# A gated-delta scan whose TensorE order is written out in the program, one product of the output projection between two blocks

## The chip, the core and the metric

The kernel runs on one core of a Trainium2 chip. The metric is device microseconds of one execution, median of several runs. TensorE multiplies (its 128x128 stationary operand is loaded by a LDWEIGHTS that the profile lists as PEld), VectorE (DVE) and ScalarE (ACT) read the results out of PSUM, GpSimd (POOL) works on SBUF alone, and SyncE (SP) issues the DMAs. Each engine works through its own instructions in the order in which they stand in the program and stops at the first that has to wait for a semaphore.

## The reference, cut to what matters

Two layers: banded attention, then gated DeltaNet, each followed by a gated output projection. The change touches only the chunked recurrence of the second layer and the projection that follows it, for 16 value heads of width 128, 64 tokens in a chunk, 33 chunks (16 tokens in the first):

```python
v_new = u - jnp.einsum('bhcd,bhdv->bhcv', w, S)
o = (jnp.einsum('bhcd,bhdv->bhcv', qc * jnp.exp(gcum)[..., None], S)
     + jnp.einsum('bhcs,bhsv->bhcv', attn, v_new))
S = S * jnp.exp(g_last)[..., None, None] + jnp.einsum('bhcd,bhcv->bhdv', k_state, v_new)
...
o = rms_norm(o, o_norm_w) * jax.nn.silu(z.reshape(B, L, DN_V_HEADS, DN_HEAD_DIM_V))
return o.reshape(B, L, DN_VALUE_WIDTH) @ w_out
```

## The kernel before

The program has four stages: projections of the attention layer, attention, projections of the DeltaNet layer, and `dn_scan`, which the change edits. The keys, values and small triangular matrices of every chunk have been written to DRAM by then.

`dn_scan` walks over 33 chunks `ng` and, within a chunk, over 4 pairs `gp` of key-head groups: 132 items, `seq`. An item passes through three stages. `stage0` multiplies the state S with keys and queries of the pair (tile `r`, two matmuls, one for each group j); POOL then scales S, DVE makes `xp` out of the key half of `r` and ACT makes `qs` out of its query half, each in four pieces (j, h). `stage1` multiplies `xp` with the inverted triangle `tp` (tile `vn`, two matmuls; the first needs the first two pieces of `xp`, the second the last two), and ACT copies it to `vs`. `stage2` makes the update of the state out of `vs` (tile `ds`, added to S by DVE) and the output (tile `o`, added to `qs` by DVE into `osb`, squared by ACT into `ssq`). After the fourth pair of a chunk `post` takes the reciprocal root on DVE (`m_o`, then ten operations on 128x8: `f_o`, `rsq_t`), scales `osb` on POOL, transposes it (tile `tp_o`, twice four) and lets DVE multiply it with z into `ot`. After two chunks (128 tokens) `ot` is complete, and a job of `out_proj` is queued: ACT and DVE split `ot` into a high and a low half (`oh`, `ol`, four parts each), 48 matmuls of 512 columns run into the tile `ps_o` (16 heads by three products, `mm3`, lines 61 to 63), and DVE adds the residual `h_t`. This is the projection's first half of columns; the second half runs after the scan from the stored `ot`. Below, a product of the projection is one of these 48 matmuls.

A step t of the loop runs `stage0` of item t, `stage1` of item t-1 and `stage2` of item t-2, and `project()` twice, each of which moves the job by one head (three products). So the code has r of item t+1 ahead of vn of item t. The tiles `vn`, `ds`, `o`, `ps_o` have one PSUM buffer, `r` has two.

The order in which instructions stand on the engines is not the order of the code: the program is built with `schedule_with_timeline_sim=True`, and the scheduler moves an instruction ahead or back on its engine wherever the data allow it.

Of the kernel before, what the change touches and what calls it, by code (L numbers as in the profile page):

```python
# [1041 lines left out]
def dn_scan(tc, a, out, sc, ident, pers):  # L1042
    nc = tc.nc
    v = nc.vector
    w_out = a["dn_w_out"][0]
    with (
        tc.tile_pool(name="pBw", reuse_waits="tile", bufs=1) as wp,
        tc.tile_pool(name="pBc", reuse_waits="tile", bufs=1) as cp,
# [20 lines left out]
        def out_proj(i, c, w, ot, tag="po"):  # L1069

            parts = []
            for q in range(4):
                oh = lp.tile([P, 4, P], F32R, tag="oh", bufs=4, name="oh2")
                ol = lp.tile([P, 4, P], F32R, tag="ol", bufs=4, name="ol2")
                split(nc, oh, ol, ot[:, q * 4:q * 4 + 4, :])
                parts.append((oh, ol))
            ht = lp.tile([P, 512], F32, tag="ht", name="h_t2")
            nc.sync.dma_start(ht, sc["h1"][NMETA + i * P:NMETA + (i + 1) * P, c * 512:c * 512 + 512])
            ps = (vpp if tag == "o" else pp).tile([P, 512], F32, tag=tag, bufs=1, name="ps_o2")
            for h in range(NV):  # L1080
                oh, ol = parts[h // 4]
# [5 lines left out]
            yield  # L1087

        S = cp.tile([P, GH, 2, P], F32, tag="S", name="S")
        nc.gpsimd.memset(S, 0.0)  # L1090
# [13 lines left out]
        def load(ng):  # L1104
# [38 lines left out]
        def stage0(ng, gp):  # L1143

            hf, n = where(ng)
            kq, bv, kt, ap, tp, osb, ssq = loaded[ng]
            gs = slice(gp * 2, gp * 2 + 2)
            if ng == 0:
                live[ng, gp] = [bv[:, gs, :], None]
                return  # L1150
            r = rpp.tile([P, 2, 2, P], F32, tag="r", bufs=2, name="r_ps")
            for j in range(2):
                nc.tensor.matmul(r[:, j], lhsT=kq[:, gp * 2 + j, :], rhs=S[:, gp * 2 + j], start=True, stop=True)  # L1153
            if ng < 32:
                for j in range(2):
                    g = gp * 2 + j
                    nc.gpsimd.tensor_tensor(S[:, g], S[:, g],  # L1157
                                            pers["eL"][hf][:, :, g, n].unsqueeze(2).to_broadcast([P, 2, P]), op=ALU.mult)
            xp = sp.tile([P, 2, P], F32, tag="xp", bufs=3, name="xp")
            qs = sp.tile([P, 2, P], F32, tag="qs", bufs=4, name="qs")  # L1160
            for j in range(2):
                g = gp * 2 + j
                for h in range(2):
                    v.scalar_tensor_tensor(xp[hb[h], j], in0=r[0:64, j, h, :], scalar=pers["c1"][hf][hb[h], g, n:n + 1],  # L1164
                                           in1=bv[hb[h], g, :], op0=ALU.mult, op1=ALU.add)
                    nc.scalar.activation(qs[hb[h], j], r[64:128, j, h, :], AF.Copy,  # L1166
                                         scale=pers["ea"][hf][hb[h], g, n:n + 1])
            live[ng, gp] = [xp, qs]

        def stage1(ng, gp):  # L1170
            tp = loaded[ng][4]
            xp = live[ng, gp][0]
            vn = vpp.tile([P, 2, P], F32, tag="vn", bufs=1, name="vn_ps")
            for j in range(2):
                nc.tensor.matmul(vn[:, j], lhsT=tp[:, gp * 2 + j, :], rhs=xp[:, j], start=True, stop=True)  # L1175
            vs = sp.tile([P, 2, P], F32, tag="vs", bufs=3, name="vs")
            nc.scalar.copy(vs, vn)
            live[ng, gp].append(vs)

        def stage2(ng, gp):  # L1180
# [3 lines left out]
            if ng < 32:  # L1184
                ds = dpp.tile([P, 2, 4, P], F32, tag="ds", bufs=1, name="ds_ps")
                for j in range(2):
                    for h in range(2):
                        nc.tensor.matmul(ds[:, h, j, :], lhsT=kt[hb[h], gp * 2 + j, :], rhs=vs[hb[h], j],  # L1188
                                         start=True, stop=True)
                v.tensor_tensor(S[:, gs], S[:, gs], ds[:, :, 0:2, :].rearrange("p h j d -> p j h d"), op=ALU.add)  # L1190
            if ng:
                ops = vpp.tile([P, 2, P], F32, tag="o", bufs=1, name="o_ps")
                for j in range(2):
                    nc.tensor.matmul(ops[:, j], lhsT=ap[:, gp * 2 + j, :], rhs=vs[:, j], start=True, stop=True)  # L1194
# [5 lines left out]
        def post(ng, gg):  # L1200
# [15 lines left out]
            for q in range(gs.start // 4, gs.stop // 4):  # L1216
                t = pp.tile([P, 8, 64], F32, tag="tp", bufs=1, name="tp_o")
                for j in range(4):
                    nc.tensor.transpose(t[:, 2 * j:2 * j + 2, :], osb[:, q * 4 + j, :], ident)
# [3 lines left out]
                yield  # L1223
            if second and gg != 0:
                nc.sync.dma_start(sc["ot"][i], ot)
                ready.append(out_proj(i, 0, w0, ot))

        ready = []
        posts = []
# [3 lines left out]
        load_wo(0, w0)  # L1233
        seq = [(ng, gp) for ng in range(33) for gp in range(GH // 2)]

        def project():
            if ready and next(ready[0], 1):
                ready.pop(0)

        LAG = 1  # L1240
        for t in range(len(seq) + 2 * LAG):
            if t < len(seq):
                ng, gp = seq[t]
                if gp == 2 and ng + 2 < 33:
                    load(ng + 2)
                stage0(ng, gp)
            project()
            if 0 <= t - LAG < len(seq):
                stage1(*seq[t - LAG])
            if 0 <= t - 2 * LAG < len(seq):  # L1250
                ng, gp = seq[t - 2 * LAG]
                stage2(ng, gp)
                if ng == 32 and gp % 2:
                    posts.append(post(ng, gp // 2))
                elif ng and gp == GH // 2 - 1:
                    posts.append(post(ng, None))
                else:
                    for _ in range(2):
                        if posts and next(posts[0], 1):
                            posts.pop(0)  # L1260
            project()
        for p in posts:
            for _ in p:
                pass
        for p in ready:
            for _ in p:
                pass

# [3 lines left out]
        w1 += [lp.tile([P, 2, 512], F32R, tag="osb", name="wo2")]  # L1272
        load_wo(1, w1)
        for i in range(NXT):
            pool, tag = ((cp, "S"), (lp, "z"), (lp, "ot"))[i % 3]
            ot = pool.tile([P, NV, P], F32, tag=tag, bufs=1, name="ot")
            nc.sync.dma_start(ot, sc["ot"][i])
            for _ in out_proj(i, 1, w1, ot, "o" if i % 2 else "po"):
                pass


# [77 lines left out]
```

## Time and profile before

| what | us |
|---|---|
| median of 3 runs (lowest, highest) | 3184.79 (3182.53, 3192.68) |
| the profiled execution | 3190.57 |
| its span | 3187.9 |
| first to last `r` (the scan's steps) | 2374.2 to 2975.2 |
| first product of the projection | 2443.1 |
| eight steps (one job of the projection) in the middle of the scan | 36.95 |

Times in the rows are microseconds from the span's start. In the view in order of time a row holds its start, its duration, the engine, the line, and written tile<-read tiles; neighbours of one kind are merged (x4 are four records), and what the engine waited for stands in brackets. A matmul of fp32 operands leaves two records, so r has four, each half of vn two, ds eight and o four. A matmul row's duration runs to the end of its result; the next matmul begins before that, and what TensorE spends on a block is the distance to the next block's start.

### The profile page before, as it was taken

How to read it: one execution, taken by the hardware profiler on the slowest of the kernel's cores; microseconds unless marked ns; L12 is line 12 of the kernel's file. 1: busy time of each engine (PE TensorE's matmuls, PEld its weight loads, DVE VectorE, ACT ScalarE, POOL GpSimd, SP SyncE). 2: the span in 40 equal slices, each digit the busy share in tenths (PEclk: the TensorE clock that was granted, in tenths of full speed). 3: DMA queues.
4: the chain of work that ended last, by engine and by line, in shares of the span. 5: the costliest groups of instructions: out<-in, count | busy, mean ns of one | idle time of the engine just before them, and what ended most of it. 6: DMA issues, size and time to landing. Idle time of an engine off the chain costs nothing.

```text
span 3187.9 us, 53874 instructions
## 1 busy us (share of the span) xinstructions
PE 2959.2 (93%) x18685; PEld 2652.4 (83%) x18685; DVE 2215.7 (70%) x5836; ACT 1453.3 (46%) x4115; POOL 966.7 (30%) x1111
## 2 busy tenths in 40 slices
PE   7999998888887999988999999999998999999899
PEld 6999996766666999988999999998986777777687
DVE  6786028889988676796654777987328888777632
ACT  5514147666665535334323535342225555555421
POOL 2001004544544323231111323222126544444200
PEclk9999999999999999999999999999998999999999
DMA  4323123222223254446542445367446676766442
GB/s 119 104 66 99 62 83 92 77 72 74 65 63 115 70 128 109 112 115 157 161 122 72 122 103 149 87 153 200 123 122 180 178 183 175 200 173 164 155 139 99
DMA packets 556696, 385.89 MB, mean 121 GB/s; under 512 B 248504, under 2 KB 508472, under 8 KB 549256
## 3 DMA queue, kind: packets, MB, share of 16 engines
q1 hardware_dynamic: 520472, 365.66, 41.2%
q10 hardware_dynamic: 35952, 16.80, 1.9%
q8 instruction: 148, 2.42, 0.3%
q14 instruction: 124, 1.02, 0.1%
HBM read 245.38 MB, written 136.97 MB: 120 GB/s over the span
## 4 chain that ended last, share of the span: by engine, by line
PE 41%; DVE 18%; DMA 4%; ACT 3%; issue 2%; SPq 1%; POOL 1%; ACTq 0%; DVEq 0%; POOLq 0%
PE ps_d L61 6%; PE ps_d L62 6%; PE ps_d L63 6%; PE ps_o L63 4%; PE ps_o L61 4%; PE ps_o L62 4%; DVE acc L769 3%; PE r_ps L1153 2%; DVE Xt L936 2%; PE ds_ps L1188 2%; DVE X L938 2%; PE o_ps L1194 1%; DVE xp L1164 1%; PE vn_ps L1175 1%; DVE wi_lo L57 1%
## 5 line engine op out<-in xcount | busy, mean ns | idle before, releaser
L61 PE MATMUL ps_d<-y_hi,wi_hi 128*128 128x384 f32 (+2 forms) x2304 | 754.9, 328 | 34.0 <-ACT u L761 29.5
L63 PE MATMUL ps_d<-y_hi,wi_lo 128*128 128x384 f32 (+2 forms) x2304 | 743.6, 323 | 0.0
L62 PE MATMUL ps_d<-y_lo,wi_hi 128*128 128x384 f32 (+2 forms) x2304 | 743.6, 323 | 0.0
L61 PEld LDWEIGHTS ps_d<-y_hi,wi_hi 128*128 128x128 f32 x2304 | 440.9, 191 | 49.0 <-ACT u L761 34.8
L63 PEld LDWEIGHTS ps_d<-y_hi,wi_lo 128*128 128x128 f32 x2304 | 440.6, 191 | 3.5 <-issue 3.3
L62 PEld LDWEIGHTS ps_d<-y_lo,wi_hi 128*128 128x128 f32 x2304 | 440.4, 191 | 3.1 <-issue 2.9
L640 POOL TENSOR_TENSOR wi_raw<-wi_raw,nw 128x1024 f32<-128x1024 f32 x96 | 207.3, 2160 | 682.3 <-DMA wi_raw<-in_dn_w_in 587.7
L769 DVE SCALAR_TENSOR_TENSOR acc<-u,cw,acc 128x1040 f32<-128x1040 f32 (+1 forms) x192 | 292.0, 1521 | 6.1
L57 DVE TENSOR_TENSOR wi_lo<-wi_raw,wi_hi 128x1024 fp32r<-128x1024 f32 x96 | 120.5, 1255 | 204.0 <-ACT wi_hi L56 195.7
L1166 ACT ACTIVATE qs<-r_ps,ea 64x128 f32<-64x128 f32 x512 | 179.5, 362 | 143.9 <-DVE xp L1164 138.3
L1164 DVE SCALAR_TENSOR_TENSOR xp<-r_ps,c,bv_t 64x128 f32<-64x128 f32 x512 | 171.9, 342 | 78.9 <-ACT qs L1166 45.8
L1157 POOL TENSOR_TENSOR S<-S,eL 128x256 f32<-128x256 f32 x248 | 162.0, 673 | 183.1 <-PE r_ps L1153 173.7
L61 PE MATMUL ps_o<-wo,oh 128*128 128x512 f32 x512 | 209.6, 409 | 3.7 <-ACT oh L56 2.9
L63 PE MATMUL ps_o<-wo,ol 128*128 128x512 f32 x512 | 205.5, 401 | 0.0
L62 PE MATMUL ps_o<-wo,oh 128*128 128x512 f32 x512 | 205.3, 401 | 0.0
L61 PE MATMUL ps_mm<-w_hi,y_hi 128*128 128x256 f32 (+1 forms) x680 | 194.1, 288 | 10.7 <-ACT y_hi L103 4.6
L63 PE MATMUL ps_mm<-w_hi,y_lo 128*128 128x256 f32 (+1 forms) x680 | 194.7, 288 | 2.0 <-DVE y_lo L104 2.0
L62 PE MATMUL ps_mm<-w_lo,y_hi 128*128 128x256 f32 (+1 forms) x680 | 193.4, 286 | 0.3 <-DVE w_lo L57 0.3
L761 ACT COPY u<-ps_d 128x384 f32<-128x384 f32 (+2 forms) x192 | 84.8, 442 | 235.9 <-PE ps_d L63 235.4
L405 ACT ACTIVATE p<-p,nb 128x272 f32<-128x272 f32 (+2 forms) x272 | 133.8, 494 | 55.5 <-DVE nb L400 55.1
L56 ACT CAST wi_hi<-wi_raw 128x1024 fp32r<-128x1024 f32 x96 | 100.6, 1048 | 118.0 <-PE ps_d L62 95.9
L57 DVE TENSOR_TENSOR ol<-ot,oh 128x512 fp32r<-128x512 f32 x128 | 89.2, 699 | 91.8 <-ACT oh L56 91.8
(306 smaller groups left out, 7110.6 us busy)
## 6 DMA issues: line engine op xcount, KB each, us to landing
wi_raw<-in_dn_w_in SPq DMA_DIRECT2D x96, 512.0 KB, 4.0
kq_t<-d_kq SPq DMA_DIRECT2D x33, 512.0 KB, 8.1
bv_t<-d_bv SPq DMA_DIRECT2D x33, 512.0 KB, 4.6
x_t<-in_x SPq DMA_DIRECT2D x32, 512.0 KB, 3.7
d_kq<-kq SPq DMA_DIRECT2D x16, 1024.0 KB, 5.3
d_bv<-bv SPq DMA_DIRECT2D x32, 512.0 KB, 4.9
kt_t<-d_ktok SPq DMA_DIRECT2D x64, 256.0 KB, 4.2
z_t<-d_z SPq DMA_DIRECT2D x16, 1024.0 KB, 6.6
```

The lines of the kernel that those rows point to most:

```text
L56: nc.scalar.copy(hi, src)
L57: nc.vector.tensor_tensor(lo, src, hi.bitcast(F32), op=ALU.subtract)
L61: nc.tensor.matmul(ps, lhsT=lh, rhs=rh, start=start, stop=False)
L62: nc.tensor.matmul(ps, lhsT=lh, rhs=rl, start=False, stop=False)
L63: nc.tensor.matmul(ps, lhsT=ll, rhs=rh, start=False, stop=stop)
L405: nc.scalar.activation(p4[:n, hh, k0:272], p4[:n, hh, k0:272], AF.Exp, bias=nb[:n, hh:hh + 1], scale=SLOPES[hg * 4 + hh], accum_out=z[:n, ...
L640: nc.gpsimd.tensor_tensor(raw, raw, nw.unsqueeze(2).to_broadcast([P, KT, P]), op=ALU.mult)
L761: nc.scalar.copy(u[:, 3 + t0:3 + t0 + n], ps[:, :n])
L769: v.scalar_tensor_tensor(acc[:, :ncol], in0=u[:, j:j + ncol], scalar=cw[:, ct, j:j + 1], in1=acc[:, :ncol], op0=ALU.mult, op1=ALU.add)
L1157: nc.gpsimd.tensor_tensor(S[:, g], S[:, g], pers["eL"][hf][:, :, g, n].unsqueeze(2).to_broadcast([P, 2, P]), op=ALU.mult)
L1164: v.scalar_tensor_tensor(xp[hb[h], j], in0=r[0:64, j, h, :], scalar=pers["c1"][hf][hb[h], g, n:n + 1], in1=bv[hb[h], g, :], op0=ALU.mult, ...
L1166: nc.scalar.activation(qs[hb[h], j], r[64:128, j, h, :], AF.Copy, scale=pers["ea"][hf][hb[h], g, n:n + 1])
```

## The change

A local `matmul` marks every matmul of the scan with `tc.keep_in_program_order` from the fifth step on: the scheduler then has to leave TensorE's order as the code has it. The code's order within a step is turned round: `stage2` of item t-2, `stage1` of t-1, `stage0` of t. `project(1)` now moves the job by one product, and stands between any two of the blocks ds, o, vn, r and the transposes; a seventh one is added while two jobs are queued. The splits are taken out of the job's start: `split_out` does a quarter of the next job whenever the current one has done another 12 products. z gets two buffers. `post` gives up its second `yield`, and its two pieces run in the first steps of the next chunk. Its first steps (t up to 3) and what follows the scan stay with the scheduler. `post`'s and `out_proj`'s arithmetic is the same, and so is the number of every instruction.

```diff
+    def matmul(out, lhsT, rhs, start=True, stop=True):
+        ins = nc.tensor.matmul(out, lhsT=lhsT, rhs=rhs, start=start, stop=stop)
+        if fixed[0]:
+            tc.keep_in_program_order(ins)
...
+            for _ in range(delay):
+                yield
...
-                mm3(nc, ps, oh[:, h % 4, :], ol[:, h % 4, :], w[h][:, 0, :], w[h][:, 1, :], h == 0, h == NV - 1)
-                if h < NV - 1:
-                    yield
+                for j, (o, hl) in enumerate([(oh, 0), (oh, 1), (ol, 0)]):
+                    matmul(ps, o[:, h % 4, :], w[h][:, hl, :], h + j == 0, h == NV - 1 and j == 2)
+                    job["done"] += 1
+                    if h < NV - 1 or j < 2:
+                        yield
...
-                zt = lp.tile([P, NV, P], F32, tag="z", bufs=1, name="z_t")
+                zt = lp.tile([P, NV, P], F32, tag="z", bufs=2, name="z_t")
...
                 v.tensor_tensor(S[:, gs], S[:, gs], ds[:, :, 0:2, :].rearrange("p h j d -> p j h d"), op=ALU.add)
+            project(1)
             if ng:
                 ops = vpp.tile([P, 2, P], F32, tag="o", bufs=1, name="o_ps")
...
+        def project(n):
+            for _ in range(n):
+                if ready and next(ready[0][1], 1):
+                    ready.pop(0)
+                if len(ready) > 1:
+                    for q in range(ready[0][0]["done"] // 12):
+                        split_out(ready[1][0], q)
+
+        for t in range(len(seq) + 2):
+            fixed[0] = t > 3
+            project(1)
+            if t >= 2:
+                stage2(*seq[t - 2])
+            project(1)
+            if 1 <= t <= len(seq):
+                stage1(*seq[t - 1])
+            project(1)
             if t < len(seq):
                 ng, gp = seq[t]
...
                 stage0(ng, gp)
-            project()
-            if 0 <= t - LAG < len(seq):
-                stage1(*seq[t - LAG])
-            if 0 <= t - 2 * LAG < len(seq):
...
+            project(1)
...
+            project(2 if len(ready) > 1 else 1)
```

On TensorE, in the middle of the scan, this stood before; the number after a name tells buffers apart, and xp_28383 is made from r_28378, which stands just ahead of these rows, xp_28444 from r_28439:

```order
L1153 MATMUL r_ps_28439<-S_26493,kq_t_27925 128x256 x2
L1194 MATMUL o_ps_28407<-vs_28338,apad_26495 128x128 x2
L1175 MATMUL vn_ps_28457<-xp_28383,tpad_26501 128x128
L1188 MATMUL ds_ps_28462<-vs_28399,kt_t_27929 128x128 x4
L1194 MATMUL o_ps_28468<-vs_28399,apad_26495 128x128 x2
L1175 MATMUL vn_ps_28457<-xp_28383,tpad_26501 128x128
L1153 MATMUL r_ps_28486<-S_26493,kq_t_28152 128x256 x2
L1175 MATMUL vn_ps_28506<-xp_28444,tpad_26501 128x128
```

The r of the next item stood ahead of both halves of an item's vn, the halves stood apart, and the projection ran in bursts elsewhere. Now the same place reads so, on TensorE (xp_28388 is made from r_28383):

```order
L1050 MATMUL r_ps_28383<-S_26493,kq_t_27928 128x256 x2
L1050 MATMUL ps_o2_28228<-wo6_26513,oh2_28118 128x512
L1050 MATMUL ps_o2_28228<-wo6_26513,ol2_28119 128x512
L1050 MATMUL ps_o2_28228<-wo7_26514,oh2_28118 128x512
L1050 MATMUL ds_ps_28416<-vs_28359,kt_t_27932 128x128 x4
L1050 MATMUL ps_o2_28228<-wo7_26514,oh2_28118 128x512
L1050 MATMUL o_ps_28423<-vs_28359,apad_26495 128x128 x2
L1050 MATMUL ps_o2_28228<-wo7_26514,ol2_28119 128x512
L1050 MATMUL vn_ps_28432<-xp_28388,tpad_26501 128x128 x2
L1050 MATMUL ps_o2_28228<-wo8_26515,oh2_28122 128x512
L1050 MATMUL r_ps_28438<-S_26493,kq_t_27928 128x256 x2
```

Between an item's r and its vn stand three products, ds, a product, o, a product, and no other r; the next r stands behind the vn. VectorE, whose order is still the scheduler's, had before, for two items (xp in pieces, S and osb of earlier items):

```order
L1164 SCALAR_TENSOR_TENSOR xp_30010<-r_ps_30005,c11_12658,bv_t_29655 64x128 x3
L1222 TENSOR_TENSOR ot_29239<-tp_o_29931,z_t_29237 128x8x64
L1164 SCALAR_TENSOR_TENSOR xp_30010<-r_ps_30005,c11_12658,bv_t_29655 64x128
L1190 TENSOR_TENSOR S_26493<-S_26493,ds_ps_30028 128x512
L1195 TENSOR_TENSOR osb_29445<-o_ps_30034,qs_29888 128x256
```

and has now, for the item of the rows above:

```order
L1186 SCALAR_TENSOR_TENSOR xp_28388<-r_ps_28383,c10_12657,bv_t_27930 64x128 x2
L1211 TENSOR_TENSOR S_26493<-S_26493,ds_ps_28416 128x512
L1186 SCALAR_TENSOR_TENSOR xp_28388<-r_ps_28383,c10_12657,bv_t_27930 64x128
L1217 TENSOR_TENSOR osb_27947<-o_ps_28423,qs_28322 128x256
L1186 SCALAR_TENSOR_TENSOR xp_28388<-r_ps_28383,c10_12657,bv_t_27930 64x128
```

S and osb moved in between the second and the fourth piece of xp. Behind the last small block of the scan stand 855 products of the projection, where 816 stood.

## Rows read from the trace of the kernel before

**Rows 1.** Tiles of the scan: records, shortest/median/longest ns, first and last start.

```profile
L1153 PE MATMUL r_ps<-S,kq_t x512: 377/379/767, 2374.2 to 2975.2; 128*128 128x256 f32 x171
...
L61 PE MATMUL ps_o<-wo,oh x512: 389/392/795, 2443.1 to 3183.2; 128*128 128x512 f32 x171
```

**Rows 2.** The chain that ended last, 2600 to 2900 us: start, us, what.

```profile
2622.16 1.10 PE r_ps L1153 x4
...
2659.11 1.10 PE r_ps L1153 x4
```

**Rows 3.** Stretches: length, busy us (PE, PEld, DVE, ACT, POOL), clock, DMA share, GB/s.

```profile
2622.16:2659.11 36.95, 35.14 (x224) 28.79 (x225) 29.50 (x81) 21.54 (x77) 18.38 (x21) 1.00 0.67 182
...
3000.00:3187.90 187.90, 181.78 (x800) 149.35 (x798) 56.42 (x84) 40.76 (x66) 0.00 (x0) 1.00 0.39 135
```

**Rows 4.** Order of time, two items of the scan, all engines.

```profile
2720.74 0.71 PE L1188 MATMUL ds_ps<-vs,kt_t 64*128 64x128 f32 x8
...
2721.38 0.71 PE L1194 MATMUL o_ps<-vs,apad 128*128 128x128 f32 x4
...
2721.57 0.69 DVE L1190 TENSOR_TENSOR S<-S,ds_ps 128x512 f32<-128x512 f32 x1 [0.34 <-PE ds_ps L1188]
...
2721.93 1.03 PE L1153 MATMUL r_ps<-S,kq_t 128*128 128x256 f32 x4
...
2722.68 0.31 ACT L1198 ACTIVATE sq_o<-osb 128x128 f32<-128x128 f32 x1 [1.06 <-DVE osb L1195]
...
2722.79 0.38 PE L1175 MATMUL vn_ps<-xp,tpad 128*128 128x128 f32 x2
...
2723.00 0.34 DVE L1164 SCALAR_TENSOR_TENSOR xp<-r_ps,c,bv_t 64x128 f32<-64x128 f32 x1 [0.41 <-PE r_ps L1153]
...
2723.19 0.19 ACT L1198 ACTIVATION_READ_ACCUMULATOR sq_o<-osb 128x1 f32 x1
...
2726.34 1.91 POOL L1115 TENSOR_TENSOR kt_t<-kt_t,wdec 128x1024 f32<-128x1024 f32 x1 [2.54 <-DVE f_o L47]
...
2726.89 1.38 DVE L45 TENSOR_TENSOR rsq_t<-f_o 128x8 f32<-128x8 f32 x1
```

**Rows 5.** Order of time: the pieces of one r, TensorE beside them.

```profile
2713.93 0.35 DVE L1164 SCALAR_TENSOR_TENSOR xp<-r_ps,c,bv_t 64x128 f32<-64x128 f32 x1 [0.46 <-ACT qs L1166]
2714.16 0.60 PE L1219 MATMUL tp_o<-ident,osb 128*128 128x128 f32 x4
2714.32 0.36 ACT L1166 ACTIVATE qs<-r_ps,ea 64x128 f32<-64x128 f32 x1 [0.42 <-DVE xp L1164]
2714.51 0.48 PE L62 MATMUL ps_o<-wo,oh 128*128 128x512 f32 x1
2714.71 0.34 DVE L1164 SCALAR_TENSOR_TENSOR xp<-r_ps,c,bv_t 64x128 f32<-64x128 f32 x1 [0.43 <-ACT qs L1166]
2714.84 0.39 PE L63 MATMUL ps_o<-wo,ol 128*128 128x512 f32 x1
```

**Rows 6.** Order of time: osb, two splits, products around o, small operations.

```profile
2706.37 0.42 DVE L1195 TENSOR_TENSOR osb<-o_ps,qs 128x256 f32<-128x256 f32 x1
...
2706.49 1.14 ACT L56 CAST oh<-ot 128x512 fp32r<-128x512 f32 x2 [0.36 <-DVE ot L1222]
...
2707.87 0.50 PE L63 MATMUL ps_o<-wo,ol 128*128 128x512 f32 x1
...
2708.21 0.60 PE L1194 MATMUL o_ps<-vs,apad 128*128 128x128 f32 x4
...
2708.57 0.48 PE L61 MATMUL ps_o<-wo,oh 128*128 128x512 f32 x1
...
2708.88 0.40 PE L62 MATMUL ps_o<-wo,oh 128*128 128x512 f32 x1
...
2709.69 0.15 DVE L45 TENSOR_TENSOR rsq_t<-f_o 128x8 f32<-128x8 f32 x1
...
2709.87 0.17 DVE L46 SCALAR_TENSOR_TENSOR rsq_t<-rsq_t,m_o 128x8 f32<-128x8 f32 x1
```

More of the change, by code (lines that the diff above doesn't have):

```diff
@@ L1067, in load_wo, with split_out, out_proj, new_job @@
                 split(nc, tiles[h][:, 0, :], tiles[h][:, 1, :], raw)
-        def out_proj(i, c, w, ot, tag="po"):
-            parts = []
-            for q in range(4):
+        def split_out(job, q):
+            if job["parts"][q] is None:
                 oh = lp.tile([P, 4, P], F32R, tag="oh", bufs=4, name="oh2")
                 ol = lp.tile([P, 4, P], F32R, tag="ol", bufs=4, name="ol2")
-                split(nc, oh, ol, ot[:, q * 4:q * 4 + 4, :])
-                parts.append((oh, ol))
+                split(nc, oh, ol, job["ot"][:, q * 4:q * 4 + 4, :])
+                job["parts"][q] = (oh, ol)
+        def out_proj(job, c, w, tag="po", delay=0):
+            i = job["i"]
+            for q in range(4):
+                if job["parts"][q] is None:
+                    split_out(job, q)
+                    delay = max(delay, 3 if fixed[0] else 0)
             ht = lp.tile([P, 512], F32, tag="ht", name="h_t2")
             nc.sync.dma_start(ht, sc["h1"][NMETA + i * P:NMETA + (i + 1) * P, c * 512:c * 512 + 512])
+            for _ in range(delay):
+                yield
             ps = (vpp if tag == "o" else pp).tile([P, 512], F32, tag=tag, bufs=1, name="ps_o2")
             for h in range(NV):
-                oh, ol = parts[h // 4]
-                mm3(nc, ps, oh[:, h % 4, :], ol[:, h % 4, :], w[h][:, 0, :], w[h][:, 1, :], h == 0, h == NV - 1)
-                if h < NV - 1:
-                    yield
+                oh, ol = job["parts"][h // 4]
+                for j, (o, hl) in enumerate([(oh, 0), (oh, 1), (ol, 0)]):
[3 more added lines that the diff above has]
+                        yield
             v.tensor_tensor(ht, ps, ht, op=ALU.add)
             nc.sync.dma_start(out[i * P:(i + 1) * P, c * 512:c * 512 + 512], ht)
-            yield
+            for _ in range(3 if fixed[0] else 1):
+                yield
+        def new_job(i, ot):
+            return dict(i=i, ot=ot, parts=[None] * 4, done=0)
         S = cp.tile([P, GH, 2, P], F32, tag="S", name="S")
@@ L1218, in post @@
                 for j in range(4):
-                    nc.tensor.transpose(t[:, 2 * j:2 * j + 2, :], osb[:, q * 4 + j, :], ident)
+                    ins = nc.tensor.transpose(t[:, 2 * j:2 * j + 2, :], osb[:, q * 4 + j, :], ident)
+                    if fixed[0]:
+                        tc.keep_in_program_order(ins)
                 hs = slice(q * 8, q * 8 + 8)
@@ L1222, in post @@
                 v.tensor_tensor(ot[:, hs, cs], t, zt[:, hs, cs], op=ALU.mult)
-                yield
+                if q + 1 < gs.stop // 4:
+                    yield
             if second and gg != 0:
                 nc.sync.dma_start(sc["ot"][i], ot)
-                ready.append(out_proj(i, 0, w0, ot))
+                job = new_job(i, ot)
+                ready.append((job, out_proj(job, 0, w0, delay=0 if i else 8)))
         ready = []
@@ L1246, in dn_scan @@
                 stage0(ng, gp)
-            project()
-            if 0 <= t - LAG < len(seq):
-                stage1(*seq[t - LAG])
-            if 0 <= t - 2 * LAG < len(seq):
-                ng, gp = seq[t - 2 * LAG]
-                stage2(ng, gp)
+            project(1)
+            if t >= 2:
+                ng, gp = seq[t - 2]
                 if ng == 32 and gp % 2:
                     posts.append(post(ng, gp // 2))
-                elif ng and gp == GH // 2 - 1:
-                    posts.append(post(ng, None))
-                else:
[L1258 to L1261, printed above, removed]
+                else:
+                    if gp != 1 and posts and next(posts[0], 1):
+                        posts.pop(0)
+                    if ng and gp == GH // 2 - 1:
+                        posts.append(post(ng, None))
+            project(2 if len(ready) > 1 else 1)
+        fixed[0] = False
         for p in posts:
@@ L1264, in dn_scan @@
                 pass
-        for p in ready:
+        for _, p in ready:
             for _ in p:
```

21 lines of the change are left out of this document (8 added, 13 removed).

## The prediction, made before the changed kernel ran

> **What bounds the kernel now.** I read the tiles first, to see where the scan lies: its steps run from the first to the last r, 2374.2 to 2975.2 us, and the projection's first product is at 2443.1, its last at 3183.2 [rows 1]. Everything that the change fixes lies between 2443.1 and 2975.2; behind that TensorE runs products and little else. Next comes the chain of waits. In the scan it passes through r again and again, and two of its r, one job of the projection apart, stand at 2622.16 and 2659.11 [rows 2]: 8 steps take 36.95 us, 4.62 a step. The busy times of just that stretch are TensorE 35.14, VectorE 29.50, ScalarE 21.54, POOL 18.38 [rows 3]. No engine is full. TensorE is nearest, but its 35.14 counts durations to the end of a result. Last is the order of time, for what a block really takes.
>
> Distances there: r holds TensorE from 2721.93 to 2722.79, .86 us, and its result is there at 1.03, so .17 after TensorE has left it; the first xp starts .04 later, at 2723.00 [rows 4]. The eight records of ds hold it .64 and are out at .71, S begins .12 behind that and takes .69 [rows 4]. The pieces of one r alternate between VectorE and ScalarE: xp at 2713.93, qs at 2714.32, xp at 2714.71, each waiting for the other in the brackets [rows 5], so .78 per pair. In the tail 800 products take 187.90 us, .235 each [rows 3]. ds to o with one product between is .34, o with one product .67 [rows 6], tp_o with one about .68 [rows 5]; so o has .43 and tp_o .45. Half of vn I put at .22, as two records of 128 columns in o. osb takes .42, two parts of oh 1.14 [rows 6]. The chain S, r, xp and qs, vn, vs, ds, S is a recurrence only for one pair, which comes round every four steps; so what decides is how many r and vn of different pairs are under way at once. Before, r of the next item stands ahead of both halves of the vn (two r buffers), and TensorE has it to do while VectorE and ScalarE are still at the four pieces.
>
> **What the change removes, adds and moves.** It removes no arithmetic. Three things move.
>
> First, the r. Now, from r to the next r, TensorE must do r, three products, ds, a product, o, a product, vn, a product. No second r is outstanding: the first half of vn needs xp 1 and 2, its second half xp 3 and 4, and the next r stands behind. From the start of vn's second half to the end of the next r it is .22 + .235 + .86 = 1.31 us, in which VectorE has no piece of xp to make.
>
> Second, S and osb stand between the pieces of xp on VectorE, and ds stands behind three products on TensorE. Take a plain step, time 0 when TensorE leaves r. xp 1 runs .21 to .55, qs 1 to .95, xp 2 .98 to 1.32. TensorE does three products and the switch to ds (.34 with a product in rows 6, so about .1 more), ds from .79, result 1.50; S 1.62, and the next operation of VectorE can begin at about 2.22: xp 3 to 2.57, qs 3 2.60 to 2.96, osb in its shadow, xp 4 2.99 to 3.33. vn's second half starts at 3.39 and the next r is left at 4.70. TensorE by itself could have had vn's second half at 2.67: it stands still .7 us, and VectorE stood still before S and behind xp 4. That is already 4.70 against the old average of 4.62, without any of the rarer work.
>
> Third, the rarer work now falls into a fixed gap, not into whatever is free. By the same walk through VectorE's and ScalarE's new orders:
> - steps with transposes (tp_o on TensorE, ot of .69 on VectorE ahead of xp 2): ds .45 later, next r at 5.14;
> - the step after, where the ten small operations of the root (.2 each, from rsq to rsq in rows 6) wait for the last pair of squares (.70 in rows 4) and hold xp 1 back, and a second ot: 5.65;
> - the step with the job's turn: two oh on ScalarE (1.14) push qs 2 to 3.14, and VectorE has S, ol, osb, ol (each 128x512 as long as S, about .69) ahead of xp 3, which starts at 4.30; with the squares ahead of qs 3: 6.96;
> - the step after that, small operations, ot, oh and ol: 5.91;
> - the step with oh, ol and h_t ahead of xp 4: 5.76; the step with two products ahead of ds: 4.48.
>
> With two plain steps, 4.70 x 2 + 5.14 + 5.65 + 6.96 + 5.91 + 5.76 + 4.48 = 43.3 us for 8 steps, 6.35 above 36.95. From 2443.1 to 2975.2 there are 532.1 / 36.95 = 14.4 such stretches: +91.4. The tail gets 855 - 816 = 39 products more, x .235 = +9.2, with no cover, since TensorE bounds there. Together +100.6. The profiled execution (3190.57) becomes about 3291; that execution lay 5.8 above the median of the three runs, so the forecast against 3184.79 is **3285 us**.
>
> How sure are the terms? The low end: if the four dear steps cost no more than a step with a transpose (5.14), 8 steps are 4.70 x 2 + 4.48 + 5 x 5.14 = 39.6, +38 for the scan and +9 behind it: 3232. The high end: small VectorE operations can be held by POOL. In the rows one rsq_t takes 1.38 us, not .15, and ends at 2728.27, within .02 of the end of kt_t on POOL (2728.25) [rows 4]. S's scaling on POOL follows every r. If one such hold of 1.2 us falls on the loop every four steps, that is 2.4 per 8 steps, x 14.4 = +35: 3320. I take the middle since every operation in it has its row.
>
> What I count at nothing: z's second buffer (its load had a whole chunk of 18.5 us as cover, half of the 36.95; without cover it would show as an ot waiting for a DMA). SP issues the same DMAs; only h_t's load goes out earlier against its products, as these are put off by three calls after the splits, so no one waits for it. The two pieces of post in the next chunk are in the walk as the steps with transposes. The wait that is added is vn's second half on xp 4: behind it on TensorE stand a product and the next r, and VectorE's xp 1, ScalarE's qs 1 and POOL's S wait for that r in turn.
>
> **The rivals.** *Interleaving fills TensorE.* If VectorE's pieces are always ready in time, a period costs what TensorE does itself: 48 products 11.3, eight r 6.9, vn 3.5, ds 5.1 with .8 for switches, o 3.5, four tp 1.8: 32.9 us. That is -4.05 x 14.4 + 9.2 = -49, or **3136**. For it: 36.95 is above 32.9, and before, the products come in bursts while the blocks stand and wait. Against it: S between xp 2 and xp 3, and only one r under way. [...]
>
> *Only the handover of xp and qs binds,* S, osb and the splits finding room beside it: .21 + 3 x .78 + .35 for the last xp + .05 to vn + 1.31 = 4.26 a step, some .2 more in the two or three steps with transposes, 34.6 for eight: -34 + 9 = **3160**. VectorE's order speaks against it, unless S is ready before xp 2 ends, which ds at .79 forbids.
>
> *Even.* The dear steps cost little, a period is 36 to 37 and the tail's +9 is all: 3175 to 3194.
>
> *Slower still,* by the holds of POOL priced above: one place, the S scaling and kt_t on POOL against VectorE's small operations and osb, decisive from about one hold in four steps, **3320**, and more if holds fall on every chunk's root. [...]
>
> *The change doesn't fix the order.* The built order of TensorE shows products one at a time between the blocks; what is not fixed is VectorE's order, and I walked the one that was built.
>
> **How the numbers follow.** A run of this kernel can be told from no change by about 0.3%, 9.6 us. Chances: forecast (3232 to 3310) .60, slower still .15, even .06, handover only .09, TensorE filled .10. Slower: .60 + .15 = .75; same .06; faster .19. The range goes from 3155, which takes in the handover rival and leaves out TensorE filled (.10), to 3345, which leaves out the worst of the holds (some .06).
>
> **What would show it.** Right: 8 steps at about 43 us in the chain; the last r near 3065, not 2975; at vn a wait for xp of about .7 us in most steps and 2 or more in the step with the job's turn; TensorE's busy share in a stretch lower than 35.14 of 36.95; single products between blocks; 39 more products, some 9 us, behind the scan. Slower still would show in rsq, osb or S rows of over a microsecond that end with a POOL row. Wrong: a period under 37, with xp 3 ahead of S's end or r following vn with no wait for xp; then the step that failed is the walk of VectorE between xp 2 and xp 3, or the .78 of a pair.

## The result, and the profile after

The changed kernel takes 3364.12 us (median of four runs, 3362.07 to 3384.52). Against the kernel before the ratio is 1.056, 95% interval 1.054 to 1.059: it is 5.6% slower. The forecast was 3285, with a range that ended at 3345. So the direction was right, but the time lies 19 us above the range: the loss was about 177 us (against 3187.33 for the kernel before in the same comparison) where 100 had been worked out.

The profiled execution took 3365.03 us, its span is 3363.3. First the tiles of the scan after the change (records, shortest, median and longest ns, first and last start), the rows that answer to [rows 1]:

```profile
L1050 PE MATMUL r_ps<-S,kq_t x512: 377/379/636, 2376.3 to 3150.1; 128*128 128x256 f32 x171
...
L1050 PE MATMUL ps_o<-wo,oh x1024: 387/389/988, 2473.4 to 3358.8; 128*128 128x512 f32 x171
```

The helper `matmul` issues all of these, so they share its line, L1050. The last r starts at 3150.1, not at 2975.2: nearly the whole loss stands ahead of it, and not in the stretch with products alone. The first product comes 30 us later than before. Three stretches of the kernel after, cut at the first r, the sixteenth r after it and the last item's r (length, then busy us of TensorE, weight loads, VectorE, ScalarE and POOL, then the granted clock, the DMA share and GB/s):

```profile
2376.26:2481.30 105.04, 71.18 (x343) 52.85 (x342) 67.38 (x153) 50.10 (x160) 57.41 (x59) 0.74 0.57 158
2481.30:3148.77 667.47, 528.29 (x3092) 409.56 (x3091) 418.39 (x1116) 318.94 (x1067) 243.70 (x280) 0.94 0.51 137
3148.77:3363.30 214.53, 206.26 (x897) 168.87 (x896) 69.48 (x119) 48.57 (x87) 1.04 (x1) 0.98 0.35 123
```

The same three of the kernel before:

```profile
2374.19:2453.04 78.85, 61.42 (x358) 48.70 (x357) 66.74 (x152) 47.73 (x153) 59.94 (x59) 0.89 0.76 196
2453.04:2974.59 521.55, 496.41 (x3123) 407.43 (x3122) 414.40 (x1106) 304.61 (x1063) 245.59 (x276) 0.99 0.65 176
2974.59:3187.90 213.31, 197.53 (x865) 161.62 (x863) 73.98 (x130) 51.33 (x99) 6.86 (x6) 0.97 0.38 132
```

The span is 175.4 us longer: 26.2 in the first sixteen steps, 145.9 in the rest of the scan, 1.2 behind it, and 2.1 ahead of it. In the first two stretches the granted clock of TensorE is lower than before, .74 against .89 and .94 against .99 (as a share of full speed; a stretch's figure is the mean).

Now eight steps in which nothing special happens, from the chain of waits of the kernel after (start, us, what), which answer to [rows 2]:

```profile
2679.24 0.86 PE r_ps L1050 x4
...
2684.50 0.86 PE r_ps L1050 x4
...
2689.83 0.86 PE r_ps L1050 x4
...
2694.64 0.86 PE r_ps L1050 x4
...
2699.47 0.86 PE r_ps L1050 x4
...
2706.42 0.86 PE r_ps L1050 x4
...
2712.55 0.88 PE r_ps L1050 x4
...
2718.44 0.88 PE r_ps L1050 x4
...
2723.03 0.86 PE r_ps L1050 x4
```

The distances are 5.26, 5.33, 4.81, 4.83, 6.95, 6.13, 5.89 and 4.59, together 43.79 us. In that order they are the step with transposes, the one with the small operations of the root, two plain steps, the step of the job's turn, the one behind it, the one with h_t, and the one with two products ahead of ds. The prediction had walked 5.14, 5.65, 4.70, 4.70, 6.96, 5.91, 5.76 and 4.48, together 43.3. The stretch as a whole, which answers to the first row of [rows 3]:

```profile
2679.08:2722.87 43.79, 35.83 (x225) 27.97 (x224) 28.13 (x81) 23.03 (x80) 17.40 (x20) 1.00 0.58 154
```

TensorE's busy time is 35.83 us where it was 35.14 in 36.95: the work is the same, the standing still is new. One plain step in order of time (start, us, engine, line, written and read tiles, and in brackets the wait):

```profile
2733.45 1.02 PE L1050 MATMUL r_ps<-S,kq_t 128*128 128x256 f32 x4
...
2735.10 0.72 PE L1050 MATMUL ds_ps<-vs,kt_t 64*128 64x128 f32 x8
2735.29 0.35 DVE L1186 SCALAR_TENSOR_TENSOR xp<-r_ps,c,bv_t 64x128 f32<-64x128 f32 x1 [0.43 <-ACT qs L1188]
...
2735.93 0.69 DVE L1211 TENSOR_TENSOR S<-S,ds_ps 128x512 f32<-128x512 f32 x1 [0.30 <-PE ds_ps L1050]
...
2736.54 0.34 DVE L1186 SCALAR_TENSOR_TENSOR xp<-r_ps,c,bv_t 64x128 f32<-64x128 f32 x1
2736.76 0.38 PE L1050 MATMUL vn_ps<-xp,tpad 128*128 128x128 f32 x2
2736.80 0.41 DVE L1217 TENSOR_TENSOR osb<-o_ps,qs 128x256 f32<-128x256 f32 x1
...
2737.31 0.35 DVE L1186 SCALAR_TENSOR_TENSOR xp<-r_ps,c,bv_t 64x128 f32<-64x128 f32 x1
...
2737.71 0.49 PE L1050 MATMUL vn_ps<-xp,tpad 128*128 128x128 f32 x2 [0.57 <-DVE xp L1186]
...
2737.95 0.48 PE L1050 MATMUL ps_o<-wo,oh 128*128 128x512 f32 x1
```

The second xp ends at 2735.64; S, which waits for ds, comes ahead of the third (2736.54), osb ahead of the fourth (2737.31), and the second half of vn waits .57 us for that; the product behind it stands that long too and begins at 2737.95, though the last oh ahead of it had been written by 2716.1. Counted from 2734.31, where TensorE leaves r if it holds it .86 us as before, S, the third and the fourth xp and vn's second half begin at 1.62, 2.23, 3.00 and 3.40; the prediction had walked 1.62, 2.22, 2.99 and 3.39. Over the whole kernel the groups of vn read (busy, mean ns, then the idle time ahead and what ended it), before and after:

```profile
L1175 PE MATMUL vn_ps<-xp,tpad 128*128 128x128 f32 x512 | 101.5, 291 | 28.3 <-DVE xp L1164 19.9 <-ACT vs L1177 8.4
```

```profile
L1050 PE MATMUL vn_ps<-xp,tpad 128*128 128x128 f32 x512 | 118.1, 314 | 171.6 <-DVE xp L1186 168.7 <-POOL S L1179 2.8
```

What the 43.79 don't hold shows in other periods; the one from 2768.41 takes 51.16. The step with the small operations there, in order of time:

```profile
2776.36 1.92 POOL L1137 TENSOR_TENSOR kt_t<-kt_t,wdec 128x1024 f32<-128x1024 f32 x1 [6.09 <-DMA kt_t<-d_ktok]
...
2776.57 1.73 DVE L47 SCALAR_TENSOR_TENSOR f_o<-rsq_t,f_o 128x8 f32<-128x8 f32 x1
...
2778.22 0.67 DVE L1211 TENSOR_TENSOR S<-S,ds_ps 128x512 f32<-128x512 f32 x1
...
2779.99 0.49 PE L1050 MATMUL vn_ps<-xp,tpad 128*128 128x128 f32 x2 [2.19 <-DVE xp L1186]
```

f_o takes 1.73 us instead of .17 and ends at 2778.30, .02 behind kt_t on POOL; S, two xp and vn stand behind it. Three steps on, in the step of the job's turn, behind another wait:

```profile
2796.60 0.79 PE L1050 MATMUL vn_ps<-xp,tpad 128*128 128x128 f32 x2 [2.24 <-DVE xp L1186]
...
2797.05 0.77 PE L1050 MATMUL ps_o<-wo,oh 128*128 128x512 f32 x1
...
2797.62 1.91 PE L1050 MATMUL r_ps<-S,kq_t 128*128 128x256 f32 x4
```

Here r takes 1.91 us, in the plain step 1.02: TensorE had stood 2.24 us ahead of vn, and the granted clock from 2796.60 to 2799.53 is .50. Not every such wait is followed by this. In the eight undisturbed steps, whose granted clock is 1.00, stands one as long:

```profile
2705.70 0.49 PE L1050 MATMUL vn_ps<-xp,tpad 128*128 128x128 f32 x2 [2.25 <-DVE xp L1186]
```

### The profile page after: what moved, and what is told of

It is laid out like the page before. It is cut to its first block, busy times and chain, and to the rows that moved or that the text cites. A ratio compares the mean times of both kernels' runs of the same rounds, so it can differ in the third digit from the quotient of the medians.

```text
span 3363.3 us, 53765 instructions
## 1 busy us (share of the span) xinstructions
PE 3013.0 (90%) x18685; PEld 2668.4 (79%) x18685; DVE 2212.0 (66%) x5836; ACT 1467.6 (44%) x4115; POOL 959.1 (29%) x1111
## 3 DMA queue, kind: packets, MB, share of 16 engines
q14 instruction: 124, 1.02, 0.1%
## 4 chain that ended last, share of the span: by engine, by line
PE 40%; DVE 19%; ACT 4%; DMA 3%; issue 3%; SPq 1%; POOL 1%; DVEq 0%; ACTq 0%; POOLq 0%
PE ps_o L1050 9%; PE ps_d L61 7%; PE ps_d L62 6%; PE ps_d L63 6%; PE r_ps L1050 4%; DVE acc L769 3%; DVE xp L1186 3%; DVE S L1211 2%; PE vn_ps L1050 2%; PE ds_ps L1050 2%; DVE Xt L936 1%; ACT qs L1188 1%; DVE X L938 1%; DVE wi_lo L57 1%; DVE ol L57 1%
## 5 line engine op out<-in xcount | busy, mean ns | idle before, releaser
L61 PE MATMUL ps_d<-y_hi,wi_hi 128*128 128x384 f32 (+2 forms) x2304 | 754.5, 327 | 30.7 <-ACT u L761 26.2
L1050 PE MATMUL ps_o<-wo,oh 128*128 128x512 f32 x1024 | 385.1, 438 | 0.9 <-DVE h_t L1103 0.9
L1188 ACT ACTIVATE qs<-r_ps,ea 64x128 f32<-64x128 f32 x512 | 186.4, 364 | 326.0 <-DVE xp L1186 321.6
L1050 PE MATMUL vn_ps<-xp,tpad 128*128 128x128 f32 x512 | 118.1, 314 | 171.6 <-DVE xp L1186 168.7
L1050 PEld LDWEIGHTS vn_ps<-xp,tpad 128*128 128x128 f32 x512 | 89.3, 199 | 203.2 <-DVE xp L1186 187.9
L1050 PE MATMUL ps_o<-wo,ol 128*128 128x512 f32 x512 | 231.5, 452 | 0.6 <-DVE ol L57 0.6
L1179 POOL TENSOR_TENSOR S<-S,eL 128x256 f32<-128x256 f32 x248 | 154.8, 643 | 265.5 <-PE r_ps L1050 265.4
L1050 PEld LDWEIGHTS ps_o<-wo,oh 128*128 128x128 f32 x1024 | 197.4, 197 | 35.7 <-ACT oh L56 1.5
L57 DVE TENSOR_TENSOR ol<-ot,oh 128x512 fp32r<-128x512 f32 x128 | 96.5, 757 | 100.5 <-ACT oh L56 100.5
```

The lines of the kernel that those rows point to most:

```text
L57: nc.vector.tensor_tensor(lo, src, hi.bitcast(F32), op=ALU.subtract)
L61: nc.tensor.matmul(ps, lhsT=lh, rhs=rh, start=start, stop=False)
L1050: ins = nc.tensor.matmul(out, lhsT=lhsT, rhs=rhs, start=start, stop=stop)
L1179: nc.gpsimd.tensor_tensor(S[:, g], S[:, g], pers["eL"][hf][:, :, g, n].unsqueeze(2).to_broadcast([P, 2, P]), op=ALU.mult)
```

## Where the 145.9 us of the scan went

I took the eight distances above as the undisturbed steps and held all 111 steps from the sixteenth r on against them. The 111 undisturbed steps would be 608.5 us (13 times 43.79, and seven of the eight steps), 86.9 over the 521.55 of before. In 15 steps over a fifth of TensorE's records have the durations of the rows at .50 (a product .77 us, not .48); these steps, below the steps at half clock, are 26.7 us longer than undisturbed ones. The other 96 are 32.3 us longer. VectorE operations that last more than .2 us over their usual duration (the lower quartile of their kind) have an excess of 26.8 us in the whole stretch, 24.5 of it in those 96 steps; below, this is the excess of long operations. So it is 86.9 of loop, 32.3 mostly of holds, 26.7 of half clock, and 26.2 for the first sixteen steps. The line between the two middle terms is rough, since a step may be at half clock for a part only. This is bookkeeping on one trace; the experiments ask whether each part goes when its cause is taken away.

## The experiments

All times are medians, to be held against 3364.12 of the changed kernel and some 3188 to 3190 of the kernel before in the same comparisons. Ratios are to the kernel before.

**One r under way, or the fixed order as such.** In the step of the loop `stage0` goes ahead of `stage1`:

```diff
-            if 1 <= t <= len(seq):
-                stage1(*seq[t - 1])
-            project(1)
             if t < len(seq):
...
                 stage0(ng, gp)
             project(1)
+            if 1 <= t <= len(seq):
+                stage1(*seq[t - 1])
+            project(1)
```

> The changed kernel with stage0 ahead of stage1 in a step: TensorE's order is still fixed, with one product between two blocks, but r of the next item stands ahead of vn, so two r are under way. Theory (the loop with only one r under way is what costs): 8 steps fall from the undisturbed 43.8 us of the changed kernel to 37 to 39, the waits of vn for xp from 169 us to under 40, the time from 3364 to between 3200 and 3280. Rival (the fixed order as such, with single products between the blocks, costs the time): 8 steps stay at 43 to 44 and the time within 20 us of 3364.

Measured: 3228.16 us, ratio 1.012 (1.009 to 1.015), 136 us less. Eight steps in the middle, and the group of vn:

```profile
2751.66:2789.30 37.64, 34.55 (x226) 27.70 (x225) 29.79 (x80) 22.06 (x76) 18.46 (x20) 1.00 0.73 179
```

```profile
L1050 PE MATMUL vn_ps<-xp,tpad 128*128 128x128 f32 x512 | 93.5, 292 | 49.2 <-DVE xp L1186 49.2
```

The order is as fixed as in the changed kernel and products stand singly between blocks, yet 8 steps take 37.64 us (36.9 to 38.6 in the later scan, up to 43.9 early in it). The rival falls. The waits of vn fell to 49, not under 40: with the second r the step of the small operations still holds vn. Two things are in the 136 us besides the loop. The granted clock of the scan behind the first sixteen steps rises to .98. And VectorE's order, which stays the scheduler's, moved with the edit: S stands ahead of the fourth xp in 97 of 109 items, where in the changed kernel it stood ahead of the third in 95. What S's place is worth by itself is asked below.

**Nothing kept in order, all other edits kept.**

```diff
-            fixed[0] = t > 3
+            fixed[0] = False
```

> The changed kernel with nothing kept in program order: code order, spread splits, z's second buffer and the shorter post stay, the scheduler orders TensorE. Theory (the fixed order alone makes it slower): 3170 to 3210, within 1% of the kernel before. Rival (the other edits, the splits spread over the scan above all, have a good part in it): over 3260.

Measured: 3194.56 us, ratio 1.002 (1.000 to 1.004). The spread splits, z's second buffer and the shorter post cost at most .4%. The loss belongs to the fixed order, as far as this order has one r under way.

**S and osb out of the way of xp.** VectorE's S and osb are queued behind the last xp that stands ahead in the code:

```diff
+                    last_xp[:] = [ins.ins]
...
-                v.tensor_tensor(S[:, gs], S[:, gs], ...)
+                with tc.issue_after(last_xp[0]) if fixed[0] and last_xp else nullcontext():
+                    v.tensor_tensor(S[:, gs], S[:, gs], ...)
...
+                with tc.issue_after(last_xp[0]) if fixed[0] and last_xp else nullcontext():
+                    v.tensor_tensor(osb[:, gs, :], ops, qs, op=ALU.add)
```

> The changed kernel with S and osb queued on VectorE behind the fourth xp instead of between the pieces; TensorE's order is untouched. Theory (the place of S and osb between the pieces of xp makes a step longer than the handover of xp and qs): the fourth xp of a plain step ends .45 us earlier, a plain step goes from 4.82 to about 4.4, 8 steps from 43.8 to 40 to 41, the time to 3310 to 3325. Rival (VectorE's whole work or TensorE's waits elsewhere set the step): a plain step of 4.7 to 4.9 and a time within 10 us of 3364.

Measured: 3349.50 us, ratio 1.050 (1.047 to 1.053), 15 us less and not the 40 to 55 expected. The plain step ahead of the job's turn did what the theory said, 4.36 us instead of 4.82, and the step of the job's turn went from 6.95 to 6.05. But 8 steps took 47.77 us, since the scheduler now put the small operations where they meet POOL. Such a step, in order of time:

```profile
2809.19 1.91 POOL L1140 TENSOR_TENSOR kt_t<-kt_t,wdec 128x1024 f32<-128x1024 f32 x1 [1.81 <-DMA kt_t<-d_ktok]
2809.20 1.92 DVE L47 SCALAR_TENSOR_TENSOR f_o<-rsq_t,f_o 128x8 f32<-128x8 f32 x1
```

The excess of long operations was 55.2 us, twice that of the changed kernel. So the next run took POOL's two large operations out of it.

**The same without POOL's two scalings.** VectorE's order is that of the run before.

```diff
-                nc.gpsimd.tensor_tensor(kt, kt, pers["wdec"]..., op=ALU.mult)
...
-            (nc.gpsimd if gg is None else v).tensor_tensor(osb[:, gs], osb[:, gs], f..., op=ALU.mult)
```

> S and osb behind the fourth xp as in s_last, and POOL's scaling of kt_t and osb left out; VectorE's order is that of s_last. Theory (s_last gains in plain steps and loses it to VectorE operations held by POOL, 55 us of them): 8 steps fall from 47.5 to 40 to 42, the time from 3350 to 3240 to 3285. Rival (the step with the small operations is long because of their count and the squares they wait for): 8 steps stay above 45 and the time above 3315.

Measured: 3265.38 us, ratio 1.025 (1.023 to 1.026). Eight steps in the middle:

```profile
2757.05:2798.61 41.56, 35.81 (x225) 27.97 (x224) 28.38 (x80) 22.47 (x77) 9.53 (x16) 1.00 0.60 164
```

They are 41.5 us nearly all along, the excess of long operations is 3.5 us, and of the steps at half clock from the sixteenth r on one is left. S's place between the xp is thus worth some 2.2 us per 8 steps (43.79 to 41.56), where 3 to 4 had been expected; the rest stays with the steps of the root and of the splits. It also bounds the price of the single r: with one r under way, S and osb behind the xp and no work of POOL to meet, 8 steps still take 41.56 us, 3.9 more than the 37.64 with two.

**The holds alone,** first with the two scalings left out of the changed kernel, by the diff just shown:

> The changed kernel without POOL's scaling of kt_t by wdec and of osb by f_o (this work is left out). Theory (VectorE operations of two SBUF inputs that are held until POOL ends lie on the loop): the long f_o and ol, 27 us over their usual durations from the first product on, become short, and the loop shortens by as much, with some of the half-clock steps behind the long waits going too: 30 to 50 us less, 3314 to 3334. Rival (the holds are covered by other waits): within 10 us of 3364.

Measured: 3323.72 us, ratio 1.042 (1.039 to 1.045), 40 us less, in the middle of what was expected. Here the scheduler also moved VectorE's operations (the step of the root takes 5.92 instead of 5.3 us), so this run is no clean price. Its quickest 8 steps take 44.3 us, so without POOL's scalings alone the undisturbed steps aren't shorter. The next does all the work, with shorter POOL operations:

```diff
-                nc.gpsimd.tensor_tensor(kt, kt, ...)
+                for g in range(0, GH, 2):
+                    nc.gpsimd.tensor_tensor(kt[:, g:g + 2], kt[:, g:g + 2], ...)
```

and in the same way four pieces of osb.

> The changed kernel with POOL's scaling of kt_t and of osb cut into four pieces of 256 elements each (all work is done). Theory (a VectorE operation of two SBUF inputs is held until the POOL operation that it meets ends, so a shorter one holds it less): the longest f_o falls from 1.9 to under .8 us, the excess behind the first product from 27 to under 15 us, the time by 10 to 30, to 3334 to 3354. Rival (VectorE is held for all the pieces in a row): the excess stays above 22 and the time within 8 us of 3364.

Measured: 3323.63 us, ratio 1.043 (1.041 to 1.044), 40 us less where 10 to 30 were expected. The excess fell from 26.8 to 8.0 us; the longest f_o was .89 us, a little over what was expected. By the bookkeeping above, 22.9 us went from the steps at full clock (32.3 to 9.4) and 15.0 from those at half clock (26.7 to 11.7); the granted clock of the scan behind the first sixteen steps is .96, not .94. By this reading the holds cost twice here: their own time in the 22.9, and a lower clock in the 15.0. VectorE's order was built anew here too, so the 40 us needn't be the holds' price alone.

**The clock.** More products, which nobody reads, stand between the halves of vn (`last` holds the tile ds of an earlier item):

```diff
+                if j == 0 and last:
+                    s = ng * 4 + gp
+                    for _ in range(8 if s < 20 or (s - 4) % 8 in (1, 4, 5, 6) else 3):
+                        matmul(last[0][:, 0, 2:4, :], w0[0][:, 0, 0:128], w0[0][:, 0, 0:256])
```

> The changed kernel with three more products of 256 columns (eight in the first steps and in those with small operations and splits) between the two halves of vn, where TensorE waits for the fourth xp; they go to a part of the tile ds that nobody reads. Theory (the clock is granted lower behind the long waits, and this costs 25 to 50 us): half-clock steps behind the first product fall from 15 to under 5, and the time by 20 to 45, to 3320 to 3344. Rival (the half clock costs little, since TensorE waits anyway, or the added products cost as much): 3355 or more.

Measured: 3342.56 us (3330.8 to 3353.0), ratio 1.049 (1.046 to 1.052), 22 us less. From the sixteenth to the 120th r no step at half clock is left, and the granted clock of the scan behind the first sixteen steps is .99 where it was .94. The first row is that stretch, the second eight undisturbed steps, with more TensorE work in the same 43.78 us:

```profile
2483.64:3118.42 634.78, 571.86 (x3706) 461.46 (x3704) 407.23 (x1114) 318.61 (x1066) 245.24 (x280) 0.99 0.54 145
2799.71:2843.49 43.78, 40.90 (x269) 33.10 (x268) 27.60 (x79) 22.47 (x77) 17.45 (x20) 1.00 0.57 150
```

So the lower clock went here when TensorE had work in its waits, and by this reading it cost some 20 us. The runs of this kernel spread more than the others', so that the price is known to about 10 us. In its trace the excess of long operations is also lower, 16.6 instead of 26.8 us; how much of the 22 us belongs to that wasn't separated.

**The start.** The order is kept only once products are there:

```diff
-            fixed[0] = t > 3
+            fixed[0] = t > 19
```

> The changed kernel with TensorE's order kept only from the twentieth step on, when products are there to stand between the blocks. Theory (the strict loop costs 26 us in the first 16 r, where no product fills the gaps and the granted clock is .59 to .83): the first 16 r take about 79 to 84 us instead of 105, the time falls by 20 to 28, to 3336 to 3344. Rival (these steps are bound by loads and POOL's work at the stage's start, whatever the order): 100 us or more, within 8 us of 3364.

Measured: 3327.14 us, ratio 1.044 (1.042 to 1.046), 37 us less, more than expected. The first sixteen steps:

```profile
2369.22:2452.01 82.79, 59.28 (x365) 45.16 (x366) 68.89 (x153) 49.49 (x159) 58.14 (x59) 0.90 0.82 210
```

They take 82.8 us, as expected, 22 less than in the changed kernel. The first r comes 7 us earlier and the rest of the scan is 10 us shorter, with an excess of long operations of 19.9 instead of 26.8; POOL's scaling of kt_t started when its load had landed (waits of 6.09 and 1.81 us for the DMA in the rows above), so which operations meet it can shift with the start; I didn't separate that further.

**Put together.** Three kernels join edits whose diffs stand above. The first has r ahead of vn, S and osb behind the fourth xp, and the late start:

> Three edits of the changed kernel together: r of the next item ahead of vn, S and osb behind the fourth xp, TensorE's order kept only from the twentieth step on. Theory (the loop of one r, the place of S and osb and the start are the costs, and they add): 8 steps of 35 to 37.5, 3165 to 3205. Rival (the held operations of VectorE take it back, as in s_last): 8 steps of 38 to 40 and 3210 or more.

Measured: 3216.31 us, ratio 1.008 (1.006 to 1.010). The rival held, with 8 steps of 38.2 to 43.7 us and an excess of 54.5 us. With two r under way, VectorE's place for S gains nothing and the excess is higher than without it (47.5). That is the next run:

> Two edits of the changed kernel: r of the next item ahead of vn, and TensorE's order kept only from the twentieth step on; VectorE's order is the scheduler's. Theory (both costs add): 8 steps of 37 to 38 in the later scan, the first 16 r in 79 to 84 us, 3200 to 3215. Rival (the early steps lose the same time later): 3222 or more.

Measured: 3209.27 us, ratio 1.007 (1.006 to 1.009); 8 steps of 37.7 us in the later scan, the first sixteen in 81.0. And with POOL's scalings in four pieces:

> rf_late with POOL's scaling of kt_t and of osb cut into four pieces each. Theory (the steps with small operations of 6.0 to 6.6 us hold a hold): these steps fall by .5 to .9, 8 steps to 36 to 36.7, the time to 3180 to 3198. Rival (holds covered): within 6 us of rf_late.

Measured: 3192.01 us, ratio 1.001 (1.000 to 1.002). Eight steps take 36.0 to 37.2 us in the later scan, partly more than the 36 to 36.7 expected; the gain over the run before is 17 us. The fixed order, repaired, is level with the scheduler's.

**The kernel before with the shorter POOL operations,** by the diff shown for the holds.

> The kernel before with POOL's scaling of kt_t and of osb cut into four pieces each. Theory (the holds, 41 us of long small operations from the 16th r on, lie partly on its path): the excess falls under 20 and the time by 5 to 25, to 3163 to 3183. Rival (with two r under way the holds are covered, or the scheduler's new order loses it): within 5 us of the kernel before.

Measured: 3168.24 us, ratio .994 (.993 to .995): 20 us faster than the kernel before, and the fastest of all that ran. Eight steps and POOL's row of osb (shortest, median, longest ns):

```profile
2702.99:2738.75 35.76, 35.12 (x226) 28.95 (x225) 28.30 (x79) 21.49 (x76) 19.57 (x32) 1.00 0.71 188
```

```profile
L1218 POOL TENSOR_TENSOR osb<-osb,f_o x124: 606/614/1392, 2413.4 to 2955.9; 128x256 f32<-128x256 f32 x124
```

The period falls from the 36.95 of [rows 2] to 35.76, although POOL is busy 19.57 us in it, not 18.38. The excess fell from 40.8 to 30.8 us only, not under 20: more operations are long (86, not 66), but by less. So the price of a hold isn't its excess; where on the loop it falls may count for more, and the scheduler's order changed with it. How much of the 20 us is the one and how much the other stays open.

## Why the prediction was right in its direction and too low in its size

**The walk of the loop held.** 43.3 us for 8 steps were worked out, 43.79 measured, and of the eight steps seven lie within .25 us of the walk (the root's step came out .3 shorter, which offsets a part of the others). In the plain step the single distances agree to .01. The forecast had +91.4 for this; the bookkeeping gives +86.9. That it is mainly the single r shows in the run with r ahead of vn: 136 us back, 37.64 us for 8 steps, the order still fixed. Of the 6.2 us between 43.79 and 37.64, 3.9 stay when S and osb stand behind the xp; the other 2.2 are S's place in a loop of one r; with two r, S's place gained nothing. One reading of a row was off without harm: the .34 of [rows 6] runs from a product to o, not from ds to o.

**The first failing step was where the change begins.** The prediction said that everything the change fixes lies between the first product and the last r. But the order is kept from the fifth step on, where the first r stands, and the first sixteen steps from there have hardly a product to put into the gaps: 9 run in them, from 2473.4 on, where 27 ran before. They cost 26.2 us that the sum counted at nothing; keeping the order later brought them from 105.0 to 82.8 us, and r ahead of vn alone to 94.7.

**The second was a term put in the wrong place.** The holds of VectorE by POOL were priced at +35 and made a rival that excludes the forecast. They don't exclude it, they come on top: 32.3 us in the bookkeeping, with 26.8 us of long operations measured. The size was about right; as a term of the sum it would have moved the forecast to 3320.

**The third was missing: the clock.** The prediction expected TensorE to stand still for 90 us or more in the scan and gave that no price beyond itself. The granted clock in the stretch behind the first sixteen steps fell from .99 to .94, steps at half clock cost 26.7 us by the bookkeeping, and with filler products all but the last two of them vanish and the time falls by 22 us. That [rows 3] shows 1.00 for the old loop says nothing about a loop that waits .6 us in a plain step and over 2 us in others. Why the clock is lower behind some of these waits and not behind others stays open: .50 stood behind one of 2.24 us, and the undisturbed eight steps have waits of .6 and 2.25 us at 1.00.

**The tail was sized too high.** +9.2 us were worked out, +1.2 measured. The products behind the scan did increase, but before, TensorE was busy 197.53 of 213.31 us there, and after, 206.26 of 214.53: the additional products went into 7.5 of the 15.8 us that it had stood. The prediction said that TensorE bounds the tail; its own row, 181.78 of 187.90 [rows 3], left room.

Together: 86.9 + 32.3 + 26.7 + 26.2 + 1.2 + 2.1 = 175.4 us, the whole difference of the spans. The forecast's 100.6 lacks 26.2, 32.3, 26.7 and 2.1 of it, and has 4.5 too much for the loop and 8.0 for the tail. The range's upper end took in the holds but neither the clock nor the start, and so ended 19 us below the time.

**The rivals on the faster side** fell as the prediction argued. TensorE's own work in 8 steps didn't become the bound (35.83 busy of 43.79), and the handover of xp and qs binds alone only in plain steps of the run with S and osb behind the xp that no hold reaches, where it gives 4.36 us (4.26 had been worked out for it). z's second buffer and the other edits cost next to nothing, as the run without any kept order shows.

## What to carry to other kernels

When an order is written out by hand, count for the engine in question how many independent chains are under way between two waits, in the old order and in the new: here one r fewer, with the place that S then got on VectorE, made 8 steps 43.8 us instead of 37.6, and no even mixing of long and short work made up for it. Walk the step through the other engines' new orders too, and add the side costs that showed here (32.3 us mostly of held operations, 26.7 us of steps at half clock), as terms of the sum and not as alternatives. And look at the stretch where the order is already fixed but the filler work isn't there yet.

## What the runs showed of the hardware that I had not expected

- f_o and ol, VectorE operations whose inputs both lie in SBUF, lasted until just past the end of POOL's two large operations when they met one, f_o up to 1.90 us (.17 is usual) and ol up to 2.34 (.68); those that read PSUM didn't. In the changed kernel's scan, from 2440 us on, 10 f_o and 7 ol began while POOL scaled kt_t or osb, over .3 us ahead of its end: every f_o ended .02 and every ol .55 us behind that end. The 57 xp, 8 ot, 7 S and 9 osb in the same place, which read PSUM, kept their usual .34, .69, .68 and .41 us.
- Shorter POOL operations went with shorter kernels: with four pieces of .61 us instead of one of 1.90 the kernel before took 20 us less and the changed one 40 us less, with more POOL time for the two scalings (157 us, not 123, and 157, not 122). Both were built anew by the scheduler, so a part of this may be the order.
- The holds cost more than their own time, by the bookkeeping: of the 38 us that the shorter POOL operations saved in the changed kernel's scan, 15.0 lay in steps at half clock.
- Products that nobody reads, put into a wait of TensorE, made the kernel faster (22 us), with a granted clock of .99 in the scan where .94 had stood.
